# A one-layer hybrid encoder block: order of the last column groups of each half, a chained fourth x block, and an earlier key fetch

## The chip, the cores and the metric

The kernel runs on one core of a Trainium2 chip. The metric is the device time of one execution in microseconds (us). Three runs of the kernel before stand beside one profiled execution of it.

## The reference, cut to what matters

`x` has 2048 rows of 1024 columns, all in float32. One layer is computed:

```python
h = rmsnorm(x, norm_w)
u = h @ w_in                                # 1024 x 5128
(a_q, a_k, a_v, a_z, g_q, g_k, g_v, g_z, g_b, g_a, r_x, r_z) = split(u)
y_a = diff_attention(a_q, a_k, a_v, ...) * silu(a_z)     # 4 heads, block-causal
y_g = gated_deltanet(g_q, g_k, g_v, g_b, g_a, g_z, ...)  # 4 heads, chunked scan
y_r = rg_lru(r_x, ...) * silu(r_z)                       # 4 blocks, scan over rows
x = x + concat(y_a, y_g, y_r) @ w_out                    # 1536 x 1024
out = rmsnorm(x, final_norm_w)
```

## The kernel before, in words

Every large product is made of three fp32r matmuls: each operand is split into a rounded part (hi) and the rest (lo), and hi\*hi, lo\*hi and hi\*lo are summed in one PSUM bank.

**Projection.** The rows are worked on in two halves of 1024 rows (`hf`), each of two blocks of 512 rows (`sb`). So there are four x blocks, 0 to 3. An x block is loaded by `load_x` as four tiles of 128 rows (`fetch_x`, line 112). `norm_x` squares them on ScalarE (line 206), computes all four scale columns at once on VectorE (lines 211 to 213 and 92 to 98), and then scales the four tiles (line 219 on GpSimd). `next_hT` transposes them on TensorE (line 277) into eight column tiles, which `h_evac` copies out of PSUM as hi on ScalarE (line 267) and lo on VectorE (line 268). The eight tiles live in the buffers "hp" (16 of them), that is two x blocks at a time. The four tiles of blocks 2 and 3 live in two buffers "big" and two buffers "bg2".

The columns of `w_in` are cut into 40 jobs a half (`half_jobs`), and a job is done for both blocks of the half; job `j` for block `sb` is a unit `(j, sb)`. A unit of 128 columns (`unit`, lines 298 to 300) has 24 matmuls of 512 columns; a unit of the attention's values (`unit_v`, lines 317 to 319) has 48 of 256 or 264 columns. Two value jobs lie at the start of a half (the pair of columns that also holds the gates b and a of the DeltaNet) and two at its end, `values(1)`. The list `order` takes the first and last pair of jobs of a half block by block, `(a, 0), (a+1, 0), (a, 1), (a+1, 1)`, and the others job by job. In the kernel before, the last four jobs of a half are 36: keys of attention head 3; 37: the gate of recurrent block 3, `Lru.outp`; 38 and 39: `values(1)`.

`Lru.gates` of a recurrent block keeps its two inputs in "big" and its scan result `m2` in a buffer "bg2"; `Lru.outp` reads `m2` for each block on VectorE (line 813), after a tanh (line 371) and a product (line 375) of its own.

The raw weights of a job come by DMA, and `split_w` makes hi on ScalarE (line 287) and lo on VectorE (line 291), all in five buffers "wx". At most two jobs have weights split at a time: `drop(j)` gives a job's weights up, and `refill` starts a generator `next_w(2)`, which waits two steps (`pump`) before it splits the next. Generators in the list `bgs` are advanced a step at a time between the matmuls of a unit.

Block 2 is loaded after unit (37, 1) of the first half; its transposes are started after (39, 0). Block 3 is loaded after (39, 1), and its transposes are queued there too.

**Attention and output.** After the projections, scores and the output projection are interleaved by a hand-written plan. `fetch_kv` reads queries, keys, values and gate of 512 rows (a key block) of one head from DRAM (lines 990 to 1006). It takes four buffers "hp" and one "sz". `all_scores` calls it ahead: key block 0 of head 0 at the first step, which is taken after unit (39, 0) of the second half, and key block 1 at the start of the second query step, after the projections. Scores (lines 1026 and 1027) go to the three PSUM banks "tp", and their maximum (line 1030) and exponential (line 1038) read them there. The output projection `out_stream` (lines 883 to 885) goes to the two banks "pj". In head 3, its sums are added to a tile read back from DRAM (line 929) by VectorE in line 956. `norm_out` sums squares over partitions in a bank "pj" as well (lines 1134 and 1135).

The kernel is built with a scheduler that follows the order of the program as a priority; an instruction whose buffer or input is not there yet can be passed by later ones. Each engine and SP's queue then runs its list in order, and waits by semaphores. A buffer is given to the next tile when all readers of the last one, also those that stand later in the program, are done.

Of the kernel before, what the change touches and what calls it, by code (L numbers as in the profile page):

```python
# [13 lines left out]
F32 = mybir.dt.float32  # L14
# [3 lines left out]
AF = mybir.ActivationFunctionType  # L18
# [5 lines left out]
P = 128  # L24
# [25 lines left out]
def tile_trunk(  # L50
# [20 lines left out]
    nc = tc.nc  # L71
# [116 lines left out]
    bgs = []  # L188
# [10 lines left out]
    def norm_x(sb, xt, pin=lambda ins: ins):  # L199

        s2 = at([P, 2, 4], "hs2", 2)
        for t, xx in enumerate(xt):
            for k in range(2):
                jk = at([P, SB], "junk", 1, BF16)
                pin(
                    nc.scalar.activation(
                        jk, xx[:, k * SB : (k + 1) * SB], AF.Square, accum_out=s2[:, k, t : t + 1]
                    )
                )
        ss = at([P, 4], "hss", 2)  # L210
        nc.vector.tensor_tensor(ss, s2[:, 0, :], s2[:, 1, :], op=ALU.add)
        rs = at([P, 4], "hrs", 2)
        nc.vector.tensor_scalar(ss, ss, 1.0 / D, 1e-6, op0=ALU.mult, op1=ALU.add)
        rsqrt(A, rs, ss, "hn")
        for t, xx in enumerate(xt):
            if sb == 1 and t < 2:
                nc.vector.tensor_scalar(xx, xx, rs[:, t : t + 1], None, op0=ALU.mult)
            else:
                nc.gpsimd.tensor_scalar(
                    xx, xx, rs[:, t : t + 1], 0.0, op0=ALU.mult, op1=ALU.add  # L220
                )
        return xt

    def load_x(sb):
        return norm_x(sb, [fetch_x(sb, t) for t in range(4)])
# [47 lines left out]
    def next_hT(hb, xt):  # L273
        for kt in range(KT):
            ps = tp()
            for t in range(4):
                nc.tensor.transpose(
                    ps[:, t * P : (t + 1) * P], xt[t][:, kt * P : (kt + 1) * P], ident
                )
            h_evac(hb, kt, slice(0, SB), ps)  # L280
            if kt % 2:
                yield
# [703 lines left out]
    def fetch_kv(hd, h, kb):  # L986
        sl = slice(kb * SB, (kb + 1) * SB)
        q = at([P, 2, SB], "hp", 16, F32R)
        for part in range(2):
            nc.sync.dma_start(  # L990
                q.bitcast(F32)[64 * part : 64 * part + 64],
                q_sp[h, part, :, sl].rearrange("(m d) s -> d m s", m=2),
            )
        hd.q[kb] = q
        for m in range(2):
            k = at([P, 2, SB], "hp", 16, F32R)
            for cp in range(2):
                nc.sync.dma_start(
                    k.bitcast(F32)[64 * cp : 64 * cp + 64],
                    k_sp[h, :, 64 * m : 64 * m + 64, sl].rearrange("t d s -> d t s"),  # L1000
                )
            hd.k[(m, kb)] = k
        hd.v[kb] = at([P, 4, 2, P], "hp", 16, F32R)
        nc.sync.dma_start(hd.v[kb].bitcast(F32), v_sp[h, :, 4 * kb : 4 * kb + 4])
        hd.z[kb] = at([P, SB], "sz", 2)
        nc.sync.dma_start(hd.z[kb], z_sp[h, :, sl])
# [123 lines left out]

    def norm_out(h, i, oo):
        o2, t1, oh, ol = oo
        pss = psum.tile([P, 256], F32, name="ss", tag="pj", bufs=2)
        nc.tensor.matmul(pss, onesr, oh, start=True, stop=False)
        nc.tensor.matmul(pss, onesr, ol, start=False, stop=True)
        nc.scalar.activation(o2, pss, AF.Ln, scale=1.0 / P, bias=epsA)
        nc.scalar.activation(o2, o2, AF.Exp, scale=-0.5)
        nc.gpsimd.tensor_tensor(t1, t1, o2, op=ALU.mult)
        yp = at([P, 2, 256], *((("xi", "gw")[i % 2], 1) if h < 3 else ("raw", 2)), F32R)
        yh, yl = yp[:, 0, :], yp[:, 1, :]  # L1140
        nc.scalar.activation(yh, t1, AF.Copy)
        nc.gpsimd.tensor_tensor(yl, t1, yh.bitcast(F32), op=ALU.subtract)
        if h == 3:
            finals.append((yh, yl))
            return
        sl = slice(i * 256, (i + 1) * 256)
        late.append(partial(nc.sync.dma_start, ya_sp[0, :, h, sl], yh.bitcast(F32)))
        late.append(partial(nc.sync.dma_start, ya_sp[1, :, h, sl], yl.bitcast(F32)))
# [7 lines left out]
    def all_scores():  # L1156
        for n, (h, i) in enumerate(steps):
            if n + 1 < len(steps):
                h2, i2 = steps[n + 1]
                if i2 % 2 == 0 and i2 > 0:  # L1160
                    fetch_kv(heads[h2], h2, i2 // 2)
            if n == 0:
                fetch_kv(heads[0], 0, 0)
                yield
            for _ in scores(heads[h], h, i, es[n]):
                yield
                if combine:
                    combine.pop(0)()
        while combine:
            yield  # L1170
            combine.pop(0)()
# [89 lines left out]

    bgs.append(start_h())

    def next_h(n, xt):
        yield from next_hT(hbs[n], xt)
        ready[n] = True

    def params():
        pps = psum.tile([P, SB], F32, name="pps", tag="tp", bufs=3)
# [31 lines left out]
    def half_jobs(hf):  # L1301
        gbs = Stage()
        gbs.ready = False
        others = []
        for h in range(4):
            r, a = Lru(hf, h), Attn(hf, h)
            others += [
                (partial(fetch_w, COL_AZ + h * P), None, a.gate),
                (partial(fetch_w, COL_RX + h * P), None, r.inp),
                (partial(fetch_w, COL_AQ + h * P), None, partial(a.qk, q_sp, 0.125)),  # L1310
                (partial(fetch_w, COL_AK + h * P), None, partial(a.qk, k_sp, 1.0)),
                (partial(fetch_w, COL_RZ + h * P), None, r.outp),
            ]

        def values(pair):
            return [
                (partial(fetch_v, pair, part, pair == 0), None, (gbs if pair == 0 else None, pair))
                for part in range(2)
            ]

        jobs = values(0)
        for h in range(4):
            g = Gdn(hf, h, gbs)
            jobs += [
                (partial(fetch_w, COL_GK + h * P), g, partial(g.key, 0)),
                (partial(fetch_w, COL_GQ + h * P), None, partial(g.key, 1)),
                (partial(fetch_w, COL_GV + h * P), None, g.val),
                (partial(fetch_w, COL_GZ + h * P), None, g.gate),
            ]
            for _ in range((4, 5, 5, 4)[h]):  # L1330
                jobs.append(others.pop(0))
        return gbs, jobs + others + values(1)

    halves = [half_jobs(hf) for hf in range(2)]
    njob = len(halves[0][1])
# [14 lines left out]
    nxt = Stage()  # L1350
# [8 lines left out]
    def refill():  # L1359
        if nxt.live < 2 and not nxt.busy and nxt.j < len(jobs):  # L1360
            nxt.busy = True
            nxt.live += 1
            bgs.append(next_w(2))

    def next_w(n):
        yield from wait(n)
        ws[nxt.j] = split_w(nxt.wr)
        nxt.j += 1
        nxt.wr = jobs[nxt.j][0]() if nxt.j < len(jobs) else None
        nxt.busy = False  # L1370
        refill()

    for j, sb in order:
        hf = j // njob
        gbs = halves[hf][0]
        if hf == 0 and 6 <= j < 18:
            k = 2 * (j - 6) + sb
            bgs.append(split_wo(k % 12, k // 12))
        _, g, post = jobs[j]
        if g is not None and sb == 0:  # L1380
            g.start()
        while not ready[2 * hf + sb]:
            pump()
        if isinstance(post, tuple):
            r, pair = post
            i = j % 2
            post_v(r, hf, pair, i, sb, unit_v(j - i, i, sb, hbs[2 * hf + sb], r is not None, (j, sb) == (0, 0)))
            if i and sb:
                drop(j)
        else:  # L1390
            while j not in ws:
                pump()
            post(sb, unit(ws[j], hbs[2 * hf + sb]))
            if sb:
                drop(j)
        pump()
        if hf == 0 and (j, sb) == (njob - 3, 1):
            xt2 = load_x(2)
        if hf == 0 and (j, sb) == (njob - 1, 0):
            hbs[2] = h_tiles()  # L1400
            bgs.append(next_h(2, xt2))
        if (j, sb) == (2 * njob - 2, 0):
            next(ost)
        if (j, sb) == (2 * njob - 1, 0):
            advance(0)
        if (j, sb) == (2 * njob - 2, 1):
            next(ost)
            advance(4)
        if (j, sb) == (njob - 1, 1):
            hbs[3] = h_tiles()  # L1410
            bgs.append(next_h(3, load_x(3)))
    while bgs:
        pump()

# [89 lines left out]
```

## Time and profile before

| what | value |
|---|---|
| three runs | 1784.29, 1788.66, 1789.12 us, median 1788.66 |
| profiled execution | 1788.15 us, its span 1786.4 us |
| TensorE busy | 1727.1 us (97%) |
| VectorE busy | 1320.6 us (74%) |
| ScalarE busy | 1001.4 us (56%) |
| GpSimd busy | 365.4 us (20%) |
| mean granted TensorE clock | 0.991 |

The profiled execution's own time is 1.75 us more than its span, and 0.5 us below the median. TensorE is the engine to watch; its idle time by stage is what the change can move. The first half's projections run to about 605 us, the second's to about 1175 us, and head 3 of the attention begins at about 1605 us.

### The profile page before, as it was taken

The page shows a single profiled execution, that of the slowest core. Times are in us where ns is not written, and L with a number is a line of the kernel's source. Part 1 is how long each engine was busy: PE and PEld are TensorE (multiplying, and loading weights), DVE is VectorE, ACT ScalarE, POOL GpSimd, SP SyncE. Part 2 cuts the span into 40 slices and gives each one's busy share as a digit, 9 for nine tenths or more (in the row PEclk, how much of TensorE's full clock was granted, in tenths as well). Part 3 has the DMA queues.
Part 4 walks back from the last instruction along what each step waited for, and adds up shares of the span by engine and source line. Part 5 has one row for each costly group of instructions (what it writes and reads, how often), then busy time and mean ns, then how long its engine had stood idle before and what let it go on. Part 6 is the DMA issues. An engine that isn't in the chain of part 4 may idle for free. (4 is left out here: it accounts for less than half of the span.)

```text
span 1786.4 us, 28581 instructions
## 1 busy us (share of the span) xinstructions
PE 1727.1 (97%) x9674; PEld 1438.5 (81%) x9674; DVE 1320.6 (74%) x3200; ACT 1001.4 (56%) x2572; POOL 365.4 (20%) x591
## 2 busy tenths in 40 slices
PE   7999999999999899999999999999999999998998
PEld 6877777888888887787888888878888888887776
DVE  5576787776786656778677668569888888787886
ACT  6524535524535452452443443469878878886784
POOL 3222521400400212031040040011212213211011
PEclk9998999999999999999999999989999999999999
DMA  6146465133135432313313324597697797596432
GB/s 182 50 125 197 139 198 162 48 101 95 57 110 163 143 83 66 92 48 101 91 52 113 88 74 123 169 270 215 198 255 201 259 258 206 163 285 186 161 135 101
DMA packets 306903, 257.47 MB, mean 144 GB/s; under 512 B 66794, under 2 KB 242116, under 8 KB 306756
## 3 DMA queue, kind: packets, MB, share of 16 engines
q1 hardware_dynamic: 306756, 255.64, 49.5%
q8 instruction: 76, 1.25, 0.3%
q14 instruction: 71, 0.58, 0.1%
HBM read 171.69 MB, written 83.89 MB: 143 GB/s over the span
## 5 line engine op out<-in xcount | busy, mean ns | idle before, releaser
L298 PE MATMUL pj<-hp,wx 128*128 128x512 f32 x1120 | 464.4, 415 | 4.9 <-DVE s L375 2.8
L300 PE MATMUL pj<-hp,wx 128*128 128x512 f32 x1120 | 444.7, 397 | 0.0
L299 PE MATMUL pj<-hp,wx 128*128 128x512 f32 x1120 | 443.5, 396 | 0.0
L300 PEld LDWEIGHTS pj<-hp,wx 128*128 128x128 f32 x1120 | 210.9, 188 | 49.6
L298 PEld LDWEIGHTS pj<-hp,wx 128*128 128x128 f32 x1120 | 211.5, 189 | 48.3 <-DVE s L375 3.4
L299 PEld LDWEIGHTS pj<-hp,wx 128*128 128x128 f32 x1120 | 212.1, 189 | 41.8
L1030 DVE TENSOR_REDUCE nm<-s 128x1 f32<-128x512 f32 (+3 forms) x320 | 191.7, 604 | 21.4 <-PE s L1027 18.6
L1038 ACT ACTIVATE s<-s,nm 128x512 f32<-128x512 f32 (+3 forms) x272 | 170.7, 629 | 50.4 <-DVE nm L1030 48.2
L363 DVE SCALAR_TENSOR_TENSOR s<-raw,pcol,s 128x512 f32<-128x512 f32 x192 | 144.7, 754 | 36.4 <-POOL s L359 34.0
L1026 PE MATMUL s<-hp 128*128 128x512 f32 (+3 forms) x320 | 125.2, 392 | 7.8 <-ACT s L1038 4.4
L291 DVE TENSOR_TENSOR wx<-wx 128x1024 fp32r<-128x1024 f32 (+1 forms) x77 | 95.9, 1246 | 46.0 <-ACT wx L287 44.6
L287 ACT ACTIVATE wx<-wx 128x1024 fp32r<-128x1024 f32 (+1 forms) x76 | 80.5, 1059 | 80.4 <-PE pj L299 73.2
L1027 PE MATMUL s<-hp 128*128 128x512 f32 (+3 forms) x320 | 118.5, 370 | 0.0
L354 POOL COPY halo<-raw 128x3 f32<-128x3 f32 x48 | 13.4, 280 | 373.3 <-ACT raw L352 364.2
L1097 PE MATMUL pt<-ident,s 128*128 128x128 f32 x544 | 84.5, 274 | 2.0 <-DVE go L1106 1.7
L1085 DVE SCALAR_TENSOR_TENSOR s<-s,cf,s 128x512 f32<-128x512 f32 (+2 forms) x112 | 74.2, 695 | 15.4 <-ACT s L1072 14.9
L883 PE MATMUL pj<-g,wx 128*128 128x512 f32 x208 | 85.4, 411 | 0.0
L596 DVE TENSOR_TENSOR tt<-tt 128x248 f32<-128x248 f32 (+30 forms) x248 | 80.0, 323 | 6.3
L590 DVE TENSOR_TENSOR tt<-lt,tt 128x248 f32<-128x248 f32 (+30 forms) x248 | 79.8, 322 | 6.6
L885 PE MATMUL pj<-g,wx 128*128 128x512 f32 x208 | 82.1, 395 | 0.0
L884 PE MATMUL pj<-g,wx 128*128 128x512 f32 x208 | 82.1, 395 | 0.0
L317 PE MATMUL pj<-wx,hp 128*128 128x264 f32 (+1 forms) x256 | 76.9, 301 | 4.0 <-ACT hp L267 1.4
(340 smaller groups left out, 4017.1 us busy)
## 6 DMA issues: line engine op xcount, KB each, us to landing
wx<-in_w_in_dram SPq DMA_DIRECT2D x78, 512.0 KB, 4.2
wx<-y_sp SPq DMA_DIRECT2D x64, 512.0 KB, 5.2
hp<-k_sp SPq DMA_DIRECT2D x64, 256.0 KB, 5.8
wo_sp<-s SPq DMA_DIRECT2D x48, 256.0 KB, 2.8
v_sp<-s SPq DMA_DIRECT2D x64, 128.0 KB, 2.9
q_sp<-s SPq DMA_DIRECT2D x32, 256.0 KB, 3.3
k_sp<-s SPq DMA_DIRECT2D x32, 256.0 KB, 4.6
y_sp<-go SPq DMA_DIRECT2D x32, 256.0 KB, 2.0
```

Of the source, the lines that this page charges most:

```text
L291: pin(eng.tensor_tensor(wl, wr, wh.bitcast(F32), op=ALU.subtract))
L298: nc.tensor.matmul(ps, wh[:, kt, :], hb[kt][:, 0, :], start=(kt == 0), stop=False)
L299: nc.tensor.matmul(ps, wh[:, kt, :], hb[kt][:, 1, :], start=False, stop=False)
L300: nc.tensor.matmul(ps, wl[:, kt, :], hb[kt][:, 0, :], start=False, stop=(kt == KT - 1))
L363: nc.vector.scalar_tensor_tensor(y, raw[:, t : t + SB], pc(wcol(t)), y, op0=ALU.mult, op1=ALU.add)
L883: nc.tensor.matmul(ps, yh, wh, start=first, stop=False)
L884: nc.tensor.matmul(ps, yh, wl, start=False, stop=False)
L1026: nc.tensor.matmul(ps[:, :n], qq, kh[:, :n], start=True, stop=False)
L1027: nc.tensor.matmul(ps[:, :n], qq, kl[:, :n], start=False, stop=True)
L1030: nc.vector.tensor_reduce(nm[:, u, m, kb : kb + 1], ps[:, :n], axis=AX.X, op=ALU.max, negate=True)
L1038: nc.scalar.activation(ee[:, :n], ps[:, :n], AF.Exp, bias=nm[:, u, m, kb : kb + 1], accum_out=zp[:, u, m, kb : kb + 1],)
L1097: nc.tensor.transpose(pt[:, off + (u - us[0]) * P : off + (u - us[0] + 1) * P], e[(u, kt // 4)][:, (kt % 4) * P : (kt % 4 + 1) * P], ident,)
```

## The change

1. The last four jobs of a half change their order: `values(1)` become jobs 36 and 37, the keys of head 3 and the gate of recurrent block 3 become jobs 38 and 39. Since `order` is written by position, the value units now go job by job, and the last four units of a half are keys, gate, keys, gate.
2. Block 3 is loaded by a generator that first transposes block 2, and is no longer loaded after the half's last unit. Of its four tiles, ScalarE scales two and GpSimd two.
3. `next_w` waits no step for the second value job of either pair, and two for the others as before.
4. Key blocks 0 and 1 of head 0 are fetched together, at the first step.
5. In head 3, `norm_out` takes its bank from "tp" and not from "pj".

```diff
@@ norm_x
             if sb == 1 and t < 2:
                 nc.vector.tensor_scalar(xx, xx, rs[:, t : t + 1], None, op0=ALU.mult)
+            elif sb == 3 and t < 2:
+                nc.scalar.activation(xx, xx, AF.Copy, scale=rs[:, t : t + 1])
             else:
@@ norm_out
-        pss = psum.tile([P, 256], F32, name="ss", tag="pj", bufs=2)
+        pss = psum.tile([P, 256], F32, name="ss", tag="pj" if h < 3 else "tp", bufs=2 if h < 3 else 3)
@@ all_scores
-                if i2 % 2 == 0 and i2 > 0:
+                if i2 % 2 == 0 and i2 > 0 and i2 // 2 not in heads[h2].q:
                     fetch_kv(heads[h2], h2, i2 // 2)
             if n == 0:
-                fetch_kv(heads[0], 0, 0)
+                for kb in range(2):
+                    fetch_kv(heads[0], 0, kb)
                 yield
@@ next_h
-    def next_h(n, xt):
-        yield from next_hT(hbs[n], xt)
-        ready[n] = True
+    def next_half(xt):
+        yield from next_hT(hbs[2], xt)
+        ready[2] = True
+        yield
+        xt = load_x(3)
+        while hbs[3] is None:
+            yield
+        yield from next_hT(hbs[3], xt)
+        ready[3] = True
@@ half_jobs
-        return gbs, jobs + others + values(1)
+        return gbs, jobs + values(1) + others
@@ refill
-            bgs.append(next_w(2))
+
+            bgs.append(next_w(0 if nxt.j % njob in (1, njob - 3) else 2))
@@ the loop over units
         if hf == 0 and (j, sb) == (njob - 1, 0):
             hbs[2] = h_tiles()
-            bgs.append(next_h(2, xt2))
+            bgs.append(next_half(xt2))
...
         if (j, sb) == (njob - 1, 1):
             hbs[3] = h_tiles()
-            bgs.append(next_h(3, load_x(3)))
```

The line `xt2 = load_x(2)` after unit (37, 1) of the first half is the same in both kernels.

## Rows read from the trace of the kernel before

**Rows 1.** The page's first part: busy time of each engine, share, instructions.
```profile
PE 1727.1 (97%) x9674; PEld 1438.5 (81%) x9674; DVE 1320.6 (74%) x3200; ACT 1001.4 (56%) x2572; POOL 365.4 (20%) x591
```

**Rows 2.** TensorE's waits over the whole span: total us, times, longest us.
```profile
PE ss L1134 <- DVE wx L956: 5.1, 5, 2.4
...
PE s L1026 <- DMA hp<-k_sp: 3.0, 3, 1.9
```

**Rows 3.** Stretches: length, busy time of each engine, granted clock, DMA share, GB/s.
```profile
2.00:8.00 6.00, 0.49 (x2) 0.43 (x3) 1.46 (x7) 2.34 (x6) 1.69 (x12) 1.00 0.96 304
604.60:639.30 34.70, 30.72 (x231) 27.92 (x230) 15.45 (x33) 15.68 (x40) 4.94 (x6) 1.00 0.46 136
1191.30:1201.20 9.90, 8.66 (x24) 7.05 (x25) 6.48 (x24) 6.28 (x22) 0.00 (x0) 0.50 1.11 258
1202.00:1240.00 38.00, 36.71 (x202) 30.06 (x201) 34.21 (x95) 36.13 (x102) 6.29 (x7) 1.00 0.79 221
```

**Rows 4.** Timeline of TensorE, 568 to 640: start, us, instruction, idle before.
```profile
568.96 0.40 PE L300 MATMUL pj<-hp,wx 128*128 128x512 f32 x1
...
585.49 0.49 PE L674 MATMUL ch<-st,g 128*128 128x128 f32 x2 [2.29 <-DVE st L694]
...
590.44 0.38 PE L277 MATMUL tp<-ident,big 128*128 128x128 f32 x2
590.66 0.38 PE L277 MATMUL tp<-ident,bg 128*128 128x128 f32 x2
...
604.91 0.39 PE L317 MATMUL pj<-wx,hp 128*128 128x264 f32 x1
...
639.33 0.50 PE L298 MATMUL pj<-hp,wx 128*128 128x512 f32 x1
```

**Rows 5.** Timeline of VectorE, 570 to 626.
```profile
570.82 0.69 DVE L813 SCALAR_TENSOR_TENSOR s<-bg,s 128x512 f32<-128x512 f32 x1
...
581.92 1.07 DVE L97 SCALAR_TENSOR_TENSOR nw_t<-nw_t,so 128x4 f32<-128x4 f32 x1
...
614.73 0.16 DVE L211 TENSOR_TENSOR hss<-hs 128x4 f32<-128x4 f32 x1 [0.18 <-ACT junk L206]
...
623.20 2.07 DVE L268 SCALAR_TENSOR_TENSOR hp<-tp,pcol,hp 128x512 fp32r<-128x512 f32 x3 [0.61 <-ACT hp L267]
```

**Rows 6.** Timeline of SP's queue, 571 to 609: fetches of x tiles.
```profile
571.58 0.33 SPq L112 DMA_DIRECT2D bg<-in_x_dram  x1
...
608.37 0.43 SPq L112 DMA_DIRECT2D bg<-in_x_dram  x1
```

**Rows 7.** Timeline of ScalarE, 575 to 611.
```profile
575.54 0.63 ACT L206 ACTIVATE junk<-bg 128x512 bf16<-128x512 f32 x1 [0.39 <-DMA bg<-in_x_dram]
...
576.85 0.19 ACT L206 ACTIVATION_READ_ACCUMULATOR junk<-bg 128x1 f32 x1
...
609.18 1.08 ACT L287 ACTIVATE wx<-wx 128x1056 fp32r<-128x1056 f32 x1
```

**Rows 8.** Timeline of GpSimd, 580 to 620.
```profile
580.76 2.22 POOL L219 TENSOR_SCALAR big<-big,hrs 128x1024 f32<-128x1024 f32 x2 [25.86 <-DVE nw_t L97]
...
617.63 2.23 POOL L219 TENSOR_SCALAR big<-big,hrs 128x1024 f32<-128x1024 f32 x2 [12.52 <-DVE hrs L98]
```

**Rows 9.** Timeline of TensorE at the start of the attention.
```profile
1191.98 0.44 PE L1026 MATMUL s<-hp 128*128 128x128 f32 x1 [1.89 <-DMA hp<-k_sp]
```

**Rows 10.** Timeline of SP's queue at the start of the attention.
```profile
1180.67 2.57 SPq L998 DMA_DIRECT2D hp<-k_sp  x4
```

**Rows 11.** Timeline of TensorE in head 3.
```profile
1637.92 0.38 PE L1134 MATMUL ss<-st,ones 128*128 128x256 f32 x1 [2.43 <-DVE wx L956]
...
1638.92 0.63 PE L883 MATMUL pj<-lt,wx 128*128 128x512 f32 x1
...
1679.82 0.38 PE L1134 MATMUL ss<-st,ones 128*128 128x256 f32 x1 [1.51 <-DVE wx L956]
...
1681.78 0.46 PE L883 MATMUL pj<-lt,wx 128*128 128x512 f32 x1
```

## The prediction

> **What bounds the kernel now.** I read the page's busy times first: TensorE is busy 97% of the span [rows 1], so a change that adds and removes no matmul can only move TensorE's idle time, 59 us of the 1786.4 in all. The view of waits then says where this change can reach. TensorE waits 5.1 us with `norm_out`'s sum because its bank "pj" is held by line 956, and 3.0 us for keys from DRAM [rows 2]. The table of stretches shows the rest [rows 3]: at the switch between the halves (604.6 to 639.3) TensorE is busy 30.7 of 34.7 us; at the start of the attention the granted clock is 0.50 (1.2 of 2.4 GHz) for 9.9 us. Last I followed the engines' timelines through the switch, looking for what each x block waits for, since the change moves the jobs about that point.
>
> **The change part by part.** *Block 2 at the switch.* The reader is to see one buffer. Block 2 needs both buffers "big" and both "bg2". One "bg2" holds the scan result of recurrent block 3 until `Lru.outp` has read it in line 813. In the trace, that line's second reading starts at 570.82 and takes 0.69 us [rows 5], and block 2's last tile is fetched at 571.58, 0.07 us later [rows 6]. The other tiles help nothing, since `norm_x` computes the scales of all four at once. In the kernel before, this reading belongs to unit (37, 1), with four more units behind it. After the change it belongs to unit (39, 1), the half's last. No unit of the next half can start before block 2 is transposed, and nothing else for TensorE is left. So the whole chain becomes idle time. Its steps, from the end of the last gate unit:
>
> - last matmul's end (568.96 + 0.40) [rows 4] to the fetch at 571.58 [rows 6]: 2.2 us
> - fetch to ScalarE's first square of the tile, which the DMA releases, 575.54 [rows 7]: 4.0
> - two squares with their sums, to 576.85 + 0.19 [rows 7]: 1.5
> - scales, without disturbance: from 614.73 [rows 5] to GpSimd's start at 617.63 [rows 8]: 2.9
> - four tiles on GpSimd, 2.23 for two [rows 8]: 4.5
> - end of that (622.1) to the first lo tile, 623.20 [rows 5]: 1.1
>
> Together 16.2 us after the end T of (39, 1). From there VectorE's lo tiles set the pace, 2.07 us for three [rows 5]: eight take 5.5 us, and the first unit is about 1.6 us slower for it.
>
> *Block 3.* Its tiles take block 2's buffers, free when the last transposes are done, at about T + 20. Four fetches of 0.43 us issue [rows 6], 2 MB in all; at the 258 GB/s of a full stretch [rows 3] they land by T + 28. Then squares 1.5, scales 2.9, scaling 2.2 (two on GpSimd while ScalarE does two; a ScalarE pass over 1056 columns took 1.08 us [rows 7]), 1.1 to the first tile: T + 35.7. TensorE, with two units of about 6.3 us and the transposes left over, comes to want it at about T + 31. So a second wait of some 4.5 us, and again 1.6 us of slow start. Two more units and 1 us of transposes end at T + 51. In the trace the same stretch runs from 604.91 to 639.33, 34.4 us [rows 4]. That is 16.5 us more. Two things come off. Block 2's 32 transposes, at 0.22 us for two [rows 4], no longer stand before T: 3.5 us. And GpSimd's scaling at 580.76 [rows 8] ran beside the scan of DeltaNet head 3: a VectorE operation on 4 elements took 1.07 us there [rows 5], against 0.16 elsewhere, and TensorE waited 2.29 us for the scan's state [rows 4]. This falls away as the scaling moves into the idle time. Net: +10.7 us. Its bounds: landing and waits are single samples; a fetch of block 3 a microsecond or two faster or slower, and the 2.29 us kept or not, make it 8 to 15.
>
> *Clock at the switch.* The rows show both: in 2 to 8 us TensorE is busy 0.5 of 6 us at a granted clock of 1.00, and behind the wait for keys 0.50 is granted for 9.9 us [rows 3], which would cost up to 5. I take +1, near the lower end: the first 3 us run at the lo tiles' pace anyway, and what the units behind them lose is covered by block 3's chain. Without that cover it is 5. The Trainium skill (TensorE: Matmul & The Clock Gate, What's actually happening) makes the slower clock the idle default, released by activity; by it the upper end would hold, while the first of the two rows disagrees and the second agrees.
>
> *Weights.* The shorter wait in `next_w` changes only the order of issue. But (38, 0) and (39, 0) now follow each other, so job 39's weights have one unit less to be fetched and split: up to 1.5 us in each half, by the 4.0 us of a fetch of the same size and two passes of 1.1; nothing if the split of 38 comes early. I take +1 for both halves.
>
> *Key blocks 0 and 1 together.* After (39, 0) of the second half the eight "hp" buffers of one x block are free, enough for two key blocks. In the trace block 1's keys are issued from 1180.67 [rows 10] and TensorE waits for them until 1191.98 [rows 9]; issued behind block 0's during the last two units, they land before they are wanted. That removes up to 3.0 us [rows 2] and, if the clock then stays up, part of the 9.9 us at half speed. ScalarE is busy 6.3 and VectorE 6.5 us in that stretch [rows 3], so no more than 3.4 us come off there: at most 6.4. Behind it ScalarE is busy 36.1 of 38 us [rows 3], so not all is kept. What is late next is the first y tile and the output weights, queued behind 2.3 MB more on SP. The gain is 0 to 6.4; I take -4.5, since those have a unit's time in hand.
>
> *`norm_out` in head 3.* Of the 2.43 us wait at 1637.92 only what stands between it and the next user of "pj" (1638.92, at half clock) can be moved ahead, about 0.5 us; the wait itself is for the sum of line 956. At 1679.82 1.96 us of work stand before the next user, so all 1.51 us go [rows 11]. With the three smaller ones 3.2 us at most of 5.1 [rows 2]. The bank "tp" is shared with the scores, so a score can now wait instead, for which no row has a price; the moved wait's own 2.4 us [rows 2] is the bound. -3.2 to +2.4; I take -2.5.
>
> Sum: 10.7 + 1 + 1 - 4.5 - 2.5 = +5.7 us on the profiled execution's 1788.15 us, which is 0.5 us below the median: 1794 us.
>
> **The rivals.** *Faster: block 2 does not wait for the gate.* If its fourth tile gets a buffer before (39, 1), for instance because the last gate units are issued earlier, block 2 has its lead of two units or more. The switch then loses its waits, up to the 4.0 us idle in the stretch [rows 3], and with 4.5 and 2.5 from the attention the time is 1777 us. Against it stands the fetch 0.07 us behind line 813 [rows 5, 6]; it decides if that fetch is issued before the half's last gate unit. Chance 0.10.
>
> *No change: the attention pays the switch back.* Keys at their bound of -6.4 and sums at -3.2 against a switch of +8 to +11: 1787 to 1790 us. For it speaks that TensorE's wait at the keys and the half clock stand one behind the other; against it the busy ScalarE. Chance 0.13.
>
> *Slower still: the clock stays low through both waits.* Block 2's wait of 16 us and block 3's of 4.5 each give up 5 us, and block 3's fetches land late: +10 to +15 more than the sum's 1, 1804 us. The trace has no wait of that length, so nothing excludes it. Chance 0.15.
>
> **How the numbers follow.** The forecast holds 0.62, with a range of its own of 1788 to 1799 from the bounds of its terms. About 0.3% (5.4 us) is what a measurement of this kernel tells from no change, and the forecast lies at that edge: I count 0.36 of it as slower, 0.26 as the same. With the third rival slower is 0.51; with 0.10 of the second the same is 0.36; the first and 0.03 of the second leave 0.13 for faster. The range 1782 to 1804 leaves out the first rival and half of the third.
>
> **What would show it.** Right: TensorE idle for about 15 us between the last gate matmul of the first half and the first 264-column matmul, the fourth x tile's fetch right behind line 813, a second wait at line 277 two units later, no wait for keys near 1190, and no `ss` wait on line 956. Wrong: a switch as short as before (first rival), a switch of more than 60 us from T to the first 512-column matmul (third), or new waits on "tp" in head 3.

## The result, and the profile after

The changed kernel takes 1799.54 us in the median of 5 runs (1794.03 to 1801.94), the kernel before 1788.66: a ratio of 1.0065, with a 95% interval of 1.0046 to 1.0083, or 11.6 us (8.2 to 14.8). It is slower. The forecast was 1794 us and "slower" with 0.51; the range of 1782 to 1804 holds the time. A later measurement of the same kernel on another chip, told below, gave 1.0033 (1.0019 to 1.0048), 5.9 us (3.4 to 8.6). The two intervals hardly meet; why the chips differ is not known.

The two profiled executions divide as follows. Landmarks are starts of TensorE instructions that both kernels have: the first 512-column matmul of the second half, the first score matmul of attention heads 1 and 3 (the 81st and 241st of 320), and the span's end. Scores run ahead of a head's other work, so head 3's first score stands at 1571.87 us in the kernel before, ahead of the 1605 us named for the head above.

| stretch | before | after | difference |
|---|---|---|---|
| start to the second half's first 512-column matmul | 639.33 | 657.46 | +18.13 |
| from there to head 1's first score | 654.98 | 652.93 | -2.05 |
| from there to head 3's first score | 277.56 | 277.41 | -0.15 |
| from there to the end | 214.57 | 210.29 | -4.28 |
| span | 1786.44 | 1798.09 | +11.65 |

Of the 18.13 us, 2.4 are there by 280 us already, before any instruction that the edit touches, and belong to these two executions; 15.7 us are the switch. Edited lines stand 2 further down than before (813 is now 815, 277 is 279, 956 is 958, 1026 is 1028).

First the switch, from the engines' timelines of the changed kernel: start, duration, instruction, and in brackets the idle time before it and what ended it. TensorE:

```profile
600.77 0.40 PE L302 MATMUL pj<-hp,wx 128*128 128x512 f32 x1
...
612.04 0.90 PE L279 MATMUL tp<-ident,big 128*128 128x128 f32 x3 [10.88 <-POOL big L221]
...
616.58 0.81 PE L319 MATMUL pj<-wx,hp 128*128 128x264 f32 x2 [0.35 <-ACT hp L269]
...
622.88 0.38 PE L279 MATMUL tp<-ident,bg 128*128 128x128 f32 x2
...
639.41 0.58 PE L279 MATMUL tp<-ident,big 128*128 128x128 f32 x3 [3.30 <-ACT big L219]
...
657.46 0.50 PE L300 MATMUL pj<-hp,wx 128*128 128x512 f32 x1
```

VectorE:

```profile
602.55 0.69 DVE L815 SCALAR_TENSOR_TENSOR s<-bg,s 128x512 f32<-128x512 f32 x1
...
608.37 0.17 DVE L211 TENSOR_TENSOR hss<-hs 128x4 f32<-128x4 f32 x1 [2.10 <-ACT junk L206]
...
614.22 1.06 DVE L96 TENSOR_TENSOR nw_t<-ro 128x4 f32<-128x4 f32 x1
```

SP's queue:

```profile
603.30 0.33 SPq L112 DMA_DIRECT2D bg<-in_x_dram  x1
...
623.00 1.88 SPq L112 DMA_DIRECT2D big<-in_x_dram  x2
```

ScalarE, then GpSimd:

```profile
606.86 0.63 ACT L206 ACTIVATE junk<-bg 128x512 bf16<-128x512 f32 x1 [1.97 <-DMA bg<-in_x_dram]
```
```profile
610.86 2.22 POOL L221 TENSOR_SCALAR big<-big,hrs 128x1024 f32<-128x1024 f32 x2 [31.20 <-issue]
```

Read it as one chain. The half's last gate matmul ends at 601.17. Line 815 reads the scan result until 603.24, and SP issues block 2's fourth tile at 603.30, 0.06 us later, as before [rows 5, 6], but now TensorE has nothing left to do. ScalarE squares the tile from 606.86, the scales begin at 608.37, GpSimd scales from 610.86, TensorE transposes from 612.04 and starts the first unit at 616.58: 15.4 us after the half's last matmul. Block 3's first fetch is issued at 623.00, just behind block 2's last transposes at 622.88, and its chain ends TensorE's second wait at 639.41.

The same stretch in the view of stretches, whose last three numbers are the granted clock, the DMA share and GB/s; behind it rows of the attention's start and of head 3:

```profile
600.00:606.00 6.00, 1.16 (x5) 0.59 (x4) 2.97 (x4) 2.20 (x3) 0.00 (x0) 0.97 0.65 209
606.00:616.00 10.00, 3.38 (x12) 2.01 (x12) 7.25 (x26) 2.81 (x11) 4.45 (x5) 0.50 0.36 109
616.00:622.00 6.00, 5.65 (x26) 5.14 (x25) 3.74 (x6) 3.74 (x6) 1.37 (x4) 0.50 0.00 0
622.00:626.00 4.00, 4.00 (x32) 4.00 (x31) 2.08 (x3) 1.37 (x2) 0.00 (x0) 0.91 0.42 142
...
1196.00:1201.00 5.00, 2.74 (x11) 2.00 (x11) 4.45 (x13) 4.12 (x10) 0.35 (x1) 0.86 1.04 298
1201.00:1206.00 5.00, 3.64 (x13) 2.72 (x12) 3.85 (x12) 4.97 (x18) 1.11 (x2) 0.50 1.10 375
1206.00:1211.00 5.00, 5.00 (x20) 4.28 (x19) 3.41 (x12) 3.92 (x13) 0.73 (x1) 0.62 1.05 382
...
1588.00:1700.00 112.00, 106.01 (x581) 87.86 (x580) 93.58 (x255) 87.74 (x250) 17.41 (x21) 1.00 0.71 216
```

And the same 112 us from head 3's first score in the kernel before:

```profile
1572.00:1684.00 112.00, 104.13 (x565) 87.38 (x564) 91.02 (x244) 84.44 (x239) 17.11 (x21) 0.97 0.69 215
```

After the wait TensorE gets 0.50 (1.2 of 2.4 GHz) until about 622, through 16 us in which it is busy for 9: all of block 2's transposes but the last few run at half speed. In the kernel before this stretch had 1.00 [rows 3].

The attention's start still has waits and a half clock, with other causes. TensorE's waits over the whole span (total us, times, longest), then two rows of its timeline at the attention's start:

```profile
PE s L1028 <- ACT s L1040: 3.7, 8, 1.3
PE pj L885 <- DVE wx L958: 3.0, 3, 1.6
...
PE av L1116 <- ACT go L1106: 1.9, 1, 1.9
...
PE ch L676 <- DVE st L696: 1.2, 2, 0.7
...
PE ss L1136 <- ACT s L1040: 0.8, 2, 0.5
```
```profile
1197.82 0.38 PE L1116 MATMUL av<-go,hp 128*128 128x256 f32 x1 [1.87 <-ACT go L1106]
...
1205.21 0.80 PE L1028 MATMUL s<-hp 128*128 128x512 f32 x1 [1.26 <-ACT s L1040]
```

No wait for keys is left, against 3.0 us before, and none of `ss` for line 958, against 5.1 us [rows 2]. But ScalarE now ends a wait of 1.87 us, and 3.0 us of waits for line 958 stand at line 885, which had none. The sum itself now waits 0.8 us for a bank "tp", behind the exponential of line 1040.

### The profile page after: what moved, and what is told of

Its sections match the earlier page's. It is cut to its first block, busy times and chain, and to the rows that moved or that the text cites. A ratio compares the mean times of both kernels' runs of the same rounds, so it can differ in the third digit from the quotient of the medians.

```text
span 1798.1 us, 28586 instructions
## 1 busy us (share of the span) xinstructions
PE 1730.6 (96%) x9674; PEld 1444.2 (80%) x9674; DVE 1318.3 (73%) x3200; ACT 1004.4 (56%) x2574; POOL 363.9 (20%) x589
## 5 line engine op out<-in xcount | busy, mean ns | idle before, releaser
L356 POOL COPY halo<-raw 128x3 f32<-128x3 f32 x48 | 13.7, 285 | 376.6 <-ACT raw L354 367.5
```

## The experiments

All times below are differences from the kernel before on the same chip: ratio times 1788.7 us, the 95% interval in brackets. Kernels of one group shared their runs of before.

**Group 1: the order.** First, the changed kernel with the old order:

```diff
-        return gbs, jobs + values(1) + others
+        return gbs, jobs + others + values(1)
...
-            bgs.append(next_w(0 if nxt.j % njob in (1, njob - 3) else 2))
+            bgs.append(next_w(0 if nxt.j % njob in (1, njob - 1) else 2))
```

> The changed kernel with the old order of the last jobs (the two jobs of values ahead of the last gate jobs no longer; the short wait for weights moved along with them). Theory A, the order is the cost: line 815's last reading has four units behind it again, block 2 has its lead, the 15.7 us that the switch lost against before come back, and the gains of head 3 (4.35 us) and of the seam into the attention (1.3 us) stay: about 1781 us (1778 to 1786), with the first 512-column matmul of the second half within 38 us of the half's last unit. Theory B, the chain of block 3 behind block 2 and ScalarE's share of its scaling are what makes the switch long: the time stays at 1796 to 1801 us.

Measured: 0.9982, -3.2 us (-5.9 to -0.5), 1782.5 us in the median. Theory A holds: with all the rest of the change in place, the order alone turns a gain into a loss. Something of B remains, though. TensorE has two waits for weights at the second half's start, 4.1 us together, which are 1.7 us in the kernel before. First this kernel, then the kernel before:

```profile
613.71 0.39 PE L319 MATMUL pj<-wx,hp 128*128 128x264 f32 x1 [2.53 <-ACT wx L289]
...
616.06 0.59 PE L321 MATMUL pj<-wx,hp 128*128 128x264 f32 x1 [1.60 <-DVE wx L293]
```
```profile
610.31 0.39 PE L317 MATMUL pj<-wx,hp 128*128 128x264 f32 x1 [1.17 <-ACT wx L287]
...
611.61 0.39 PE L319 MATMUL pj<-wx,hp 128*128 128x264 f32 x1 [0.54 <-DVE wx L291]
```

Next the converse, the kernel before with nothing but the line `jobs + values(1) + others`.

> The kernel before with nothing but the new order of the last jobs. Theory A: the same wait at the switch as after the change, without the half of block 3 on ScalarE, so block 3 comes some 2 us later still, and without the gains of the attention: 15.7 to 20 us above before, 1802 to 1809 us. Theory B: 1786 to 1792 us, because block 3's fetches are not chained and GpSimd scales it alone as before.

Measured: 1.0108, +19.3 us (16.6 to 22.0), median 1804.5. The order alone costs more than the whole change. From the half's last matmul to the second half's first 512-column matmul it takes 57.3 us (56.3 in the changed kernel), with the same two waits, 10.92 and 3.18 us.

Then a dose: `others[::-1]` in the changed kernel's order, so that the gate comes one job ahead of the keys.

> The changed kernel with its last two jobs exchanged: the gate of the recurrent part comes ahead of the keys of attention head 3, so line 815's last reading has one unit of about 6.3 us behind it. Theory A predicts a dose: block 2's chain starts one unit earlier against the end of the half, TensorE's gap shrinks from 10.9 to about 5 us, and the time falls by 4 to 7 us to 1793 to 1796 us; at the end of the second half the gate's tanh and table load are no longer last, so the wait of 1.9 us at the first output product may go too, by 0 to 2 us more. Theory B: no change at the switch, 1797 to 1801 us.

Measured: 1.0053, +9.5 us (6.6 to 12.3). The direction is right, the dose too small: the stretch is 53.8 us, 2.5 less, and the wait at line 279 is still 9.83 us. Line 815 starts at 591.66, 2.8 us ahead of the end of the half's last matmul instead of 1.4 behind it, so the chain had 4.2 us of start. It lost much of that on its way, as the timelines of SP, ScalarE and VectorE show:

```profile
592.42 0.33 SPq L112 DMA_DIRECT2D bg<-in_x_dram  x1
```
```profile
597.95 0.63 ACT L206 ACTIVATE junk<-bg 128x512 bf16<-128x512 f32 x1 [2.87 <-DMA bg<-in_x_dram]
```
```profile
601.61 1.26 DVE L293 TENSOR_TENSOR wx<-wx 128x1056 fp32r<-128x1056 f32 x1
602.79 0.15 DVE L98 SCALAR_TENSOR_TENSOR hrs<-nw_t,hrs 128x4 f32<-128x4 f32 x1
```

From its fetch to its first square the tile took 5.5 us instead of 3.6, with a weight fetch just ahead and others behind it, and a split of weights stood on VectorE between the last two steps of the scales. A chain that is moved into work shares its engines.

**Group 2: the one buffer, the attention's parts, and the clock.** A buffer of its own for block 2's fourth tile does not fit: the pool would take 207.6 kB in each partition, and 204.8 are left. So in the changed kernel only this tile goes into another buffer that exists already:

```diff
-        xx = at([P, D], *(... else ("big", 2) if t < 2 else ("bg2", 2)))
+        xx = at([P, D], *(... else ("big", 2) if t < 2 else ("lt", 1) if (sb, t) == (2, 3) else ("bg2", 2)))
```

> The changed kernel, in which only the fourth tile of x block 2 goes elsewhere: into the buffer of lt, free between DeltaNet head 3 of the first half and head 0 of the second, so that it need not wait for line 815. Theory A, that one buffer is the cost of the new order: the tile is fetched two units ahead with the other three, TensorE's gap of 10.9 us at line 279 goes and with it the half clock; 4.5 us of the 15.7 may stay, the wait for weights that the chained fetches of block 3 showed with the old order: 1782 to 1789 us. Theory B, the new order costs for another reason (weights of the last job, block 3's buffers): 1794 to 1801 us.

Measured: 0.9991, -1.6 us (-4.1 to 0.7), median 1786.2. So this one buffer is what the new order costs at the switch. Between the profiles 13.7 us come back there (the table at the end of this section), between the ratios 7.5 to 13, by which of the changed kernel's two is taken. Line 279 waits no longer than 0.9 us, and the stretch from the half's last matmul is 38.2 us. But the same dependence has moved to the next tile. TensorE's and SP's timelines:

```profile
608.52 0.59 PE L319 MATMUL pj<-wx,hp 128*128 128x264 f32 x1 [6.58 <-ACT wx L289]
```
```profile
600.91 0.33 SPq L112 DMA_DIRECT2D bg<-in_x_dram  x1
601.29 0.43 SPq L126 DMA_DIRECT2D wx<-in_w_in_dram  x1
```

Block 3's fourth tile now waits for line 815 at 600.91, and on SP the second half's second weights stand behind it, so that TensorE waits 6.58 us for those.

The keys alone, on the kernel before:

```diff
-                if i2 % 2 == 0 and i2 > 0:
+                if i2 % 2 == 0 and i2 > 0 and i2 // 2 not in heads[h2].q:
...
-                fetch_kv(heads[0], 0, 0)
+                for kb in range(2):
+                    fetch_kv(heads[0], 0, kb)
```

> The kernel before, with key blocks 0 and 1 fetched together and nothing else. If the fetch itself is worth what the profile of the old order shows (offset from 4.5 to 0.4 us over the start of the attention), the time falls by 4 us, to 1781 to 1784 us. Rival: those 4 us came from something else in that kernel, ScalarE waits in place of the keys as after the change, and the time falls by 0 to 1.5 us, 1785 to 1787 us.

Measured: 0.9978, -3.9 us (-6.1 to -1.8), median 1784.7: the fetch is worth it.

Keys and the bank "tp" (the change's line in `norm_out`), no other part:

> The kernel before with the keys together and the sums of head 3 in the bank tp; the order of jobs, the chain and ScalarE's share stay as before. If the two parts add up, 2.5 to 4.4 us less than with the keys alone: 1777 to 1781 us, which is also below the kernel with only the order undone (1782.5 us). Rival: in head 3 the scores that wait for the bank give back what the sums gain, 1781 to 1784 us.

Measured: 0.9961, -7.0 us (-9.8 to -3.9), median 1782.0. This is the version that beats both kernels. The parts add up: 3.0 us more than the keys alone, though the two intervals overlap.

Now the clock. Behind the half's last unit of the changed kernel:

```diff
         if (j, sb) == (njob - 1, 1):
+            pk = psum.tile([P, SB], F32, name="pk", tag="tp", bufs=3)
+            for n in range(40):
+                nc.tensor.matmul(pk, onesr, hbs[1][KT - 1][:, 0, :], start=n == 0, stop=n == 39)
             hbs[3] = h_tiles()
```

> The changed kernel with 40 matmuls of 512 columns, whose sums nobody reads, behind the half's last unit, so that TensorE works for some 9 us of the 10.9 us that it waits at line 279. Theory A, about 5 of the switch's 15.7 us are the half clock that follows the wait: the granted clock is 1.00 when the transposes and the first units of the next half run, and the time falls by 3 to 6 us, to 1793 to 1797 us. Theory B, those units run at the pace of VectorE's lo tiles and of block 3's chain anyway, so that the clock costs 1 us as forecast: 1797.5 to 1801 us, with a second wait at line 279 that is longer by what the units gain.

Measured: 1.0077, +13.8 us (10.4 to 17.2). The test missed its place: the matmuls stand at 620.98, behind block 2's transposes, with which they share the bank "tp" (in another bank, below, they stand ahead of them), and the wait of 10.8 us is unfilled. What it does show is slack: 9.6 us of work put between the two waits made the stretch 60.2 instead of 56.3 us, and the second wait fell from 3.30 to 1.54 us. TensorE still waits there although it had 9.6 us more to do, so block 3's chain, not TensorE's own work, sets the end of the second wait.

**Group 3: the filling in its place, and what is left over.** The same 40 matmuls in bank "pj" (`tag="pj", bufs=2`):

> The changed kernel again with 40 matmuls of 512 columns whose sums nobody reads (9.4 us), now written to the bank pj, so that they stand between the half's last unit and block 2's first transpose and fill the wait at line 279. Theory A, half clock after the wait is 4 to 5 us of the switch's 15.7: the granted clock is 1.00 from the first transpose on, and the time is 6 to 9 us above before, against 11.6 of the changed kernel. Theory B, block 3's chain sets the end of the stretch, so that faster units only wait longer at the second gap: 10 to 13 us above before, the second wait at line 279 longer than 3.3 us.

Measured: 1.0022, +3.9 us (1.4 to 6.3). The matmuls fill 596.88 to 606.4; 1.51 us of the wait remain, and the granted clock still falls to 0.50, from about 611 to 616. The stretch is 53.6 us. So useless work made this kernel faster than the changed one, by 2.7 us between two profiles of the switch and by 7.7 us between two ratios from different chips; group 4 is about that difference. Of the 2.7 us only 0.8 stand ahead of block 3's fetches: block 2's last transposes start 20.9 us behind the half's last unit, against 21.7.

Two parts of the change added to the best version, one at a time. ScalarE's half of block 3's scaling (the change's `elif sb == 3 and t < 2`):

> The kernel before with keys together and the bank tp (7.0 us below before), and with half of block 3's scaling on ScalarE, neither chained nor with the new order. Theory A, ScalarE's share is harmless or helps, since block 3's lo tiles start 2.2 us sooner: 6.5 to 9 us below before. Theory B, two passes of 2.2 us stand on ScalarE ahead of the split of the next weights, as line 289 ended TensorE's wait with the old order and the chain: 3 to 5 us below before.

Measured: 0.9972, -5.0 us (-7.3 to -2.7), at the edge of theory B; the interval reaches into both.

Block 3 chained behind block 2 (the change's `next_half`, with GpSimd scaling both):

> The same kernel of 7.0 us below before, with block 3 chained behind block 2 instead of ScalarE's share. With the order undone the changed kernel was 3.2 us below before, 3.8 less than this one without chain, share and short waits. Theory A, the chain is those 3.8 us, because its four fetches stand on SP ahead of the second values' weights: 3 to 4.5 us below before, with a wait for line 287 near 613 of some 4 us in two parts. Theory B, it is ScalarE's share: 6 to 8 us below before.

Measured: 0.9967, -5.9 us (-8.8 to -3.0). Waits for weights of 2.41 and 1.73 us stand at 608 and 611 as expected, but the price is not separated from zero. Both kernels lie above the one without these parts and below the changed kernel with the order back; all the intervals overlap. What is shown is where the chain makes TensorE wait, not how many microseconds each part costs.

**Group 4: the clock once more.** With 50 instead of 40 matmuls in bank "pj":

> As the last keep-busy kernel, with 50 instead of 40 of the matmuls that nobody reads (11.7 us), the last ones between the first transposes. With 40, TensorE still waited 1.5 us and then ran at 0.50 for about 6 us. Theory A, the clock is what the filling gives back: no half clock before the first units of the next half, from the half's last matmul to the first of 512 columns at most 53 us (56.3 in the changed kernel, 53.8 with 40), and the time is 2 to 4 us below that with 40. Theory B, the rest of the stretch belongs to VectorE's lo tiles and block 3's chain: the same stretch is 53.5 to 55 us, and the time is that with 40 or up to 2 us above it.

Measured: 1.0033, +5.9 us (3.6 to 8.2). The switch and the time disagree. TensorE's timeline and the stretches of this kernel:

```profile
600.77 10.43 PE L1422 MATMUL pk<-hp,ones 128*128 128x512 f32 x44
611.82 0.55 PE L279 MATMUL tp<-ident,big 128*128 128x128 f32 x3 [0.62 <-POOL big L221]
...
620.21 0.38 PE L279 MATMUL tp<-ident,bg 128*128 128x128 f32 x2
...
634.27 0.55 PE L279 MATMUL tp<-ident,big 128*128 128x128 f32 x3 [2.60 <-ACT big L219]
```
```profile
606.00:611.00 5.00, 5.00 (x23) 3.84 (x21) 2.66 (x20) 2.66 (x10) 0.36 (x1) 1.00 0.73 209
611.00:616.00 5.00, 3.80 (x19) 2.05 (x18) 4.48 (x7) 0.49 (x1) 4.31 (x5) 1.00 0.00 0
616.00:621.00 5.00, 4.48 (x35) 4.10 (x36) 4.51 (x7) 4.46 (x8) 1.21 (x4) 1.00 0.01 3
```

Here the clock never falls before block 3: counted from the end of the half's last unit, block 2's last transposes start 2.4 us sooner than in the changed kernel, block 3's first ones 4.9, and the stretch is 51.9 us. So the switch is as short as theory A asked, with 4.4 us given back, but not all of it is shown to be the clock's. The 2.4 us are block 2's transposes at full instead of half speed. The next 2.5 lie in block 3's fetches. From the end of block 2's last transposes to ScalarE's first square of block 3's fourth tile it takes 8.0 us here and 10.5 in the changed kernel. ScalarE's line of this kernel, then of the changed one:

```profile
628.61 0.63 ACT L206 ACTIVATE junk<-bg 128x512 bf16<-128x512 f32 x1
```
```profile
633.78 0.63 ACT L206 ACTIVATE junk<-bg 128x512 bf16<-128x512 f32 x1
```

In the kernels with the order alone and with the gate first the clock fell to 0.50 behind the first wait too, and this part took 8.8 and 9.2 us. So the slow fetches are not shown to follow from the clock, and their cause stays open.

And the changed kernel itself, on the same chip:

> The changed kernel itself, on the chip and in the rounds of the keep-busy kernel, since 40 matmuls gave 2.5 us between two profiles of the switch and 7.7 us between two ratios taken on different chips. If the ratios are right, it is 10 to 13 us above before and 6 to 8 above the kernel with filling; if the profiles are, 5 to 8 us above before and 2 to 3 above the kernel with filling.

Measured: 1.0033, +5.9 us (3.4 to 8.6), with a median of 1796.1 us over 12 runs (1789.5 to 1805.9); the filled kernel had 1793.2. The reading by the profiles fits better: the 7.7 us between chips were mostly no effect of the filling. What the filling gives in the whole time is 0 to 3 us by these numbers, which the intervals do not tell from nothing. Its profiled stretch at the switch was 58.6 us, with the clock at 0.50 behind both waits.

**Two stretches in all profiles.** Job 34 starts at the same place of a half in every kernel, and the jobs that change their order stand behind it. The first column of numbers runs from the first matmul of job 34 in the first half to the second half's first 512-column matmul, the second from that of job 34 in the second half to head 1's first score, both in us:

| kernel | over the switch | into the attention |
|---|---|---|
| before | 126.7 | 206.5 |
| old order: keys alone | 127.9 | 201.7 |
| old order: keys and bank | 129.4 | 201.6 |
| the same with ScalarE's share | 129.0 | 203.0 |
| the same with the chain | 129.9 | 202.6 |
| changed kernel, order back | 131.2 | 202.4 |
| new order alone | 143.4 | 206.2 |
| changed kernel, two profiles | 142.4, 144.8 | 205.3, 206.1 |
| gate first | 139.9 | 205.4 |
| another buffer | 128.7 | 205.3 |
| 40 matmuls in "tp", in "pj" | 146.3, 139.7 | 205.3, 205.7 |
| 50 matmuls in "pj" | 138.0 | 208.9 |

The first three kernels are the same at the switch, so their 126.7 to 129.4 us show how far single profiles differ there. The second column shows what the whole time hides: fetched together, the keys give 3.4 to 4.9 us with the old order, and 1.2 at most with the new one.

## Why the prediction came out as it did

The mechanism was right, and of the five signs that it named all five are there: some 15 us from the half's last matmul to the first unit (10.9 of them in one wait), the fetch right behind the line that was 813, a second wait at the transposes two units later, no wait for keys, no `ss` wait for line 958. One sign of the other list is there as well, but small: the 0.8 us that sums in head 3 wait for a bank "tp". By its terms:

- **Block 2's chain**, 16.2 us forecast: 15.4. Every step was within 0.4 us of its row. The buffer as its cause is shown by the kernel with another buffer, which gave 13.7 us of the switch back.
- **Transposes and scan wait that move away**, -3.5 and -2.29, together -5.8: borne out. From job 34 to the half's last matmul it is 92.3 us before and 86.1 after, 6.1 less. VectorE's operations on 4 elements are at 1.06 us again beside GpSimd's scaling (614.22), but TensorE waits no more than 0.2 us for them now, and no wait for the scan's state is longer than 0.7 us in the profile's list of waits.
- **The clock at the switch**, +1 forecast: the step that failed. The argument was that block 3's chain covers what the units lose at half speed. But that chain begins when block 2's last transposes free the buffers, and those ran at half speed too: against the kernel that keeps TensorE at 1.00 they start 2.4 us later. The clock fell a second time behind the second wait. The text's upper bound of 5 us is not shown either: the whole stretch differs by 4.4 us in one profile of the changed kernel and by 6.7 in the other (51.9 against 56.3 and 58.6), but what goes beyond 2.4 us lies mostly in the next term. The row in which 0.5 of 6 us had been busy at a clock of 1.00 [rows 3] was from the start of the program. It was the wrong neighbour, and the matmuls that follow it did not run at full speed (the last section shows it), so it did not speak for a cheap clock. By the Trainium skill (TensorE: Matmul & The Clock Gate, What's actually happening) throttled is the default and activity releases it. Behind this 10.9 us wait the trace agrees, with 0.50 for about 16 us, and so do the slow matmuls at the start.
- **Block 3's fetches**, 8 us from T + 20 to T + 28: mis-sized for the changed kernel, where the fourth tile is squared 10.5 us behind the last transposes (10.3 in its second profile). The kernel with 50 matmuls had 8.0. Why they are slower is open. Without both, the stretch is nearly as forecast: 51.9 us against T + 51.
- **Weights of job 39**, +1: nothing. No wait of a 512-column matmul for split weights is in the list.
- **Keys**, -4.5: -3.9 (-6.1 to -1.8) alone, so well sized with the old order. But the sum took the terms as independent, and they are not: in the changed kernel's profile only 2.05 us come off between the switch and head 1, and from job 34 on only 1.2. The wait for keys went, but 1.87 and 1.26 us of waits for ScalarE came, and the clock fell to 0.50. The new order, which puts the gate's work at the end of the half as well, takes the gain back: the table's five kernels with the old order and the keys together got 3.4 to 4.9 us. What in the order does it stays open. With the gate a job earlier the wait at line 1116 is 0.2 instead of 1.9 us, yet the stretch is no shorter.
- **The bank "tp"**, -2.5: 4.28 us in this profile, 3.0 between the two ratios. All waits of TensorE in head 3 that the list has sum to 10.2 us before and 7.9 after: 5.1 at `ss` are gone, 3.0 are new at line 885, where the unfinished line 958 is now met, and 0.8 at `ss` for the bank. The scores' own waits for line 1040 did not grow; they fell from 3.2 to 1.1 us. The granted clock did the rest or part of it: over the 112 us from head 3's first score it is 1.00 in all eleven profiles with the sums in "tp", and 0.97 in all three without.

By the profiles, the changed kernel is 9.2 us slower than before (15.7 - 2.05 - 0.15 - 4.28), where 5.7 was forecast. At the switch 12.7 was forecast with clock and weights; the clock's 1.4 us and the fetches' 2.5 too little and the weights' 1 too much leave 0.1 of the difference. In the attention the keys came out 2.4 us too small and the bank 1.8 too large, so that its two terms nearly make up the forecast -7.0 (-6.3, and -7.0 in the version that has just these). The first ratio's 11.6 us and the second's 5.9 lie on either side of 9.2. That the second meets the forecast's 5.7 so well is in part luck, since single terms are off by up to 2.5 us.

The first rival's condition, a buffer for block 2's fourth tile ahead of the half's last gate unit, is what the kernel with the buffer of lt made. It did not bring the 1777 us: 1.6 us below before, since the wait passed to block 3's tile and, in SP's queue, to the weights behind it, and since beside the new order the keys gave little (205.3 against 206.5 us in the table). The third rival ("slower still: the clock stays low through both waits", 1804 us) was the forecast's own mechanism with the clock at a higher price. The second profile of the changed kernel took 1805.9 us, but not by that mechanism: its stretch of 58.6 us stayed short of the rival's 60, and of the 6.1 us that its span is longer than the first profile's, 2.4 lie at the switch and 3.9 in the second half's projections. Its other 11 runs took 1789.5 to 1800.1 us.

## What to carry to other kernels

When work is reordered, list for each buffer the last reader, not the last writer: here one read of 0.69 us, moved to the end of a phase, held a fetch and 15.4 us of work on four engines behind it. A transfer taken out of that wait passes it on to whatever stands behind the next one in the same queue, so follow the queue once more. Charge an idle stretch of TensorE as long as this one with the half clock behind it, above all when the slow work itself frees the next buffers: here 2.4 us, while the stretch between landmarks differed by 4.4 to 6.7. And measure a gain together with the other parts: the keys' 3.4 to 4.9 us shrank to 1.2 at most beside the new order.

## What the runs showed of the hardware

The time of one and the same kernel goes with its granted clock. In group 2 the 29 runs of before go from 1794.05 us at a mean granted clock of 0.987 to 1782.52 at 0.995: 12 us, more than most parts of this change are worth. Nor does one wait fix it: behind the same wait of 1.83 us for ScalarE at the start of the attention, the changed kernel with the old order got 0.53 in the 5 us that begin 3.5 us after the wait, and the best version 1.00 throughout. These are two kernels, so the pair alone leaves the reason open:

```profile
1187.00:1192.00 5.00, 5.00 (x22) 4.41 (x22) 4.36 (x18) 4.47 (x17) 0.72 (x1) 0.53 1.10 380
```
```profile
1186.00:1191.00 5.00, 3.97 (x21) 2.77 (x21) 4.63 (x20) 5.00 (x18) 0.73 (x1) 1.00 1.02 315
```

The first row is of the kernel with the order back, the second of the best version. A gain of 2 or 3 us is therefore read from a short stretch between landmarks, in more than one profile, and the whole time is left to many runs.

At the start of this program the granted clock of the profile does not hold. In the kernel before it is 1.00 from 0 to 40 us. But until 16.7 us the matmuls of 264 columns take 0.42 us or more and start at least 0.22 us apart; from 17.3 on they take 0.28 to 0.29 us, and back to back they start 0.13 us apart. The 0.42 us are also what such a matmul takes at 0.50 behind the changed kernel's first wait (at 618.50 and 619.79):

```profile
16.48 0.42 PE L319 MATMUL pj<-wx,hp 128*128 128x264 f32 x1
16.70 0.42 PE L317 MATMUL pj<-wx,hp 128*128 128x264 f32 x1
...
17.27 0.29 PE L317 MATMUL pj<-wx,hp 128*128 128x264 f32 x1
17.40 0.28 PE L318 MATMUL pj<-wx,hp 128*128 128x264 f32 x1
```
